# Scores in quarter tiles, a reordered first mixer, 64-column sample products and a third rotation buffer in a two-layer streaming encoder

## The chip, the cores and the metric

The kernel runs on one core of one Trainium2 chip. The core has TensorE (PE; its weight loads are listed as PEld), VectorE (DVE), ScalarE (ACT), GpSimd (POOL) and SyncE (SP). The kernel issues all its DMAs from SP. The metric is device time in microseconds (us) from start to end of one execution; lower is better.

## The reference

One inference step of a two-layer encoder over 1024 prompt frames and 32 sample frames, 1024 features wide. Cut to what matters:

```python
def run_trunk(x, pos, hgrn_state, cache_k, cache_v, ...):
    for layer in range(2):
        h = rms_norm(x, norm_mix_pre[layer])
        if layer == 0:                                   # first mixer
            q, f, i, g = split(h @ w_a_in)               # 4 x 1024 columns
            forget = lb + (1 - lb) * sigmoid(f)
            o, S = hgrn2_scan(silu(q), 1 - forget, i, log(forget), hgrn_state)   # 8 heads
            mix = (rms_norm(o) * silu(g)) @ w_a_out
        else:                                            # second mixer
            k, v = split(rms_norm(x, kv_norm) @ w_kv); k = rope(k, pos)
            q = rope(h @ w_b_q, pos)                     # 16 query heads, 4 key heads
            p = softmax(q @ k / 8 over own and two earlier chunks of 64 keys, with sinks)
            mix = (p @ v) @ w_b_out
        x = x + rms_norm(mix, norm_mix_post[layer])
        a, b = split(rms_norm(x) @ w_ffn_in[layer])      # 2 x 2816
        x = x + rms_norm((silu(a) * b) @ w_ffn_out[layer])
```

A chunk has 64 frames, so a query sees 192 keys: its own chunk and two before it. The outputs are both frame streams, the mixer's states and the newest 128 keys and values.

## The kernel before

**Frames and numbers.** The 1056 frames are three blocks of columns, b = 0, 1, 2, with W = 384, 384 and 288. The last 32 columns of block 2 are the sample. Dense products are made of three: each operand is split into a rounded part and its remainder (`xh`, `xl`, `wh`, `wl`), and xh·wh, xl·wh and xh·wl are summed in PSUM in one accumulation. `wunit` loads 128x1024 weights into `wst` (two buffers), ACT casts them to `wh` (line 102, or 98 with a scale), and DVE subtracts to get `wl` (line 103 or 99).

**Two dense forms.** `mm_fm` (line 141) has weights stationary and W frames moving: 24 matmuls for 128 features. `mm_tm` (line 153) has up to 128 frames stationary and 256 weight columns moving: 24 matmuls. Block 2 calls it for 128, 128 and 32 frames. Products land in the PSUM tag `mm`, which has four slots.

**First mixer.** It starts with `xload(0)`, which casts the first block and sums its squares; `rnorm` (lines 188 and 163 to 171) turns the sums into `rb`, a reciprocal root taken in ten small steps on ACT and DVE; `rcol` (line 201) turns `rb` into columns `rt`. `vproj` and `gproj` make the values and gates with `mm_tm`. For each head, `stage_a` makes F and Q, `stage_b` decays on DVE and POOL, `stage_c` the scores, `states` the states (its transposes `pt`, line 958, need POOL's line 941), `outputs` the outputs. After a block's last gates `oback` transposes all eight heads (`pgt`, line 1026, two PSUM slots); ACT and DVE empty them (lines 1028 and 1029).

**Second mixer.** `rope` makes two products and rotates them on DVE (lines 1129 to 1132) and POOL (1133, 1134) into a tile `ra` with two buffers, which then goes to DRAM as `kd` (keys) or `qd` (queries). `kproj(2)` also writes the two key outputs `out_kp` and `out_ks` from `ra` (lines 1158 and 1159). Attention has 12 units for each block (4 key heads, 3 pieces of 128 frames). A unit is `att_s` (scores, line 1273; row maximum, exponentials), `att_t` (six transposes `ptp`, lines 1333 and 1342) and `att_v` (values, lines 1355 and 1370). A query piece holds two chunks. The keys they share are scored with both chunks as 128 stationary columns, the other 64 keys of each with 64. Between the units stand fillers: late `qproj`s in block 0, `outproj` (output product, norm, next norm) of blocks 0 and 1 in blocks 1 and 2; `postnorm` of block 0 rereads its rows from DRAM (`xo<-xsc`, line 278).

**Order.** The program's text gives priorities; a scheduling layer that weighs costs of its own decides what stands where in each engine's queue, and pools wait for their buffers. An engine works its queue in order.

Of the kernel before, what the change touches and what calls it, by code (L numbers as in the profile page):

```python
# [59 lines left out]
def build(nc, tc, I, O):  # L60
# [82 lines left out]

    def mm_tm(ps, rows, units, xh, xl, t0):
        n = 24
        i = 0
        for u, (wh, wl) in enumerate(units):
            for k in range(4):
# [34 lines left out]

    def rnorm(acc, dst, W, ps=None):
# [5 lines left out]
        rsqrt(dst[:, :W], ps[:, :W], v[:, :W], t[:, :W], ps[:, :W], D,  # L190
              lambda o, x: nc.scalar.activation(o, x, AF.Square),
# [458 lines left out]
    def outproj(b, arr, pre, w2, xold, wnext, spill, ahead=None):  # L650
# [5 lines left out]
        for k in range(KT):  # L656
# [7 lines left out]
            mm_fm(ps, W, units, (k % 2) * 128, lambda q: oh[:, q, :], lambda q: ol[:, q, :])  # L664
# [18 lines left out]
    with tc.tile_pool(name="hp", bufs=1) as hp, \  # L683
# [4 lines left out]
        def xload(b, mid=None):  # L688
# [5 lines left out]
            for k in range(KT):  # L694
# [9 lines left out]
                put_x(b, k, xo[:, :W], xs[b], "mix_pre0")  # L704
                sq_acc(acc, W, xo[:, :W], k == 0)
# [5 lines left out]
            rcol(rb, W, r, hps.tile([128, 512], F32, tag="hs", name="hs", bufs=1) if b == 0 else None)  # L711

        xl0 = xload(0, lambda: first_units.append(wunit(I["wfq"][1])))
# [13 lines left out]
        state = [None] * 8  # L727

        def vproj(p, b, ahead=0):
# [4 lines left out]
            for jl in range(3):  # L734
                rows = min(128, W - jl * 128)
                ps = mmps()
                mm_tm(ps, rows, units, xs[b][0], xs[b][1], jl * 128)
# [7 lines left out]
        v0 = vproj(0, 0, 1)  # L745

        def gproj(p, b):
            units = wpair("wg", p)
            W = BL[b][1]
            for jl in range(3):  # L750
                rows = min(128, W - jl * 128)
                ps = mmps()
                mm_tm(ps, rows, units, xs[b][0], xs[b][1], jl * 128)
# [15 lines left out]
        def stage_a(c, h, b):  # L769
# [16 lines left out]
            if h == b == 0:  # L786
                go(xl0)
                go(v0, 2)
# [251 lines left out]
        for b in range(NB):  # L1040
# [9 lines left out]
            for h in range(8):  # L1050
# [5 lines left out]
                go(ga)  # L1056
                go(gs)
# [9 lines left out]
                if b > 0 and h == 1:  # L1067
                    oback(b - 1)
# [42 lines left out]
    def rope(b, units, res):  # L1111
# [3 lines left out]
        mm_fm(pA, W, units, 0, lambda k: xh[:, k, :], lambda k: xl[:, k, :])  # L1115
        yield
        pB = mmps()
        mm_fm(pB, W, units, 128, lambda k: xh[:, k, :], lambda k: xl[:, k, :])
# [8 lines left out]
        a = rp[0].tile([128, 2, 384], F32, tag="ra", name="ra", bufs=2)  # L1127
# [18 lines left out]
    def kproj(b, units):  # L1146
# [8 lines left out]
        if b < 2:  # L1155
            kload(b)
        else:
            nc.sync.dma_start(O["kp"], a[:, :, 128:256])
            nc.sync.dma_start(O["ks"][:, :, 96:128], a[:, :, 256:288])

    def vproj1(b, units):
# [3 lines left out]
        for jl in range(3):  # L1165
            rows = min(128, W - jl * 128)
            ps = mmps()
            mm_tm(ps, rows, units, xh, xl, jl * 128)
# [16 lines left out]
    def qproj(b, g, units):  # L1185
# [366 lines left out]
```

## Time and profile before

| | us |
|---|---|
| three runs | 2492.41, 2497.97, 2497.51 (median 2497.51) |
| profiled execution | 2499.08 |
| its span, first to last instruction | 2496.6 |
| PE busy in the span | 2426.9 (97%) |
| DVE, ACT, POOL busy | 1695.8 (68%), 1124.0 (45%), 245.5 (10%) |

The profile is of one execution. Its time exceeds its span by 2.5 us, which lie before and after it. A matmul is written with its stationary size (rows*columns) and its moving operand (partitions x columns). Matmuls overlap in the array, so a matmul's duration is not its cost; the distance from one start to the next is. A group's busy time is the time in which at least one of it ran. The granted clock (PEclk) is a share of 2.4 GHz: 0.50 is the lower of the two levels, 1.2 GHz.

### The profile page before, as it was taken

The page shows a single profiled execution, that of the slowest core. Times are in us where ns is not written, and L with a number is a line of the kernel's source. Part 1 is how long each engine was busy: PE and PEld are TensorE (multiplying, and loading weights), DVE is VectorE, ACT ScalarE, POOL GpSimd, SP SyncE. Part 2 cuts the span into 40 slices and gives each one's busy share as a digit, 9 for nine tenths or more (in the row PEclk, how much of TensorE's full clock was granted, in tenths as well). Part 3 has the DMA queues.
Part 4 walks back from the last instruction along what each step waited for, and adds up shares of the span by engine and source line. Part 5 has one row for each costly group of instructions (what it writes and reads, how often), then busy time and mean ns, then how long its engine had stood idle before and what let it go on. Part 6 is the DMA issues. An engine that isn't in the chain of part 4 may idle for free.

```text
span 2496.6 us, 45627 instructions
## 1 busy us (share of the span) xinstructions
PE 2426.9 (97%) x17964; PEld 2361.4 (95%) x17964; DVE 1695.8 (68%) x3733; ACT 1124.0 (45%) x2467; POOL 245.5 (10%) x477
## 2 busy tenths in 40 slices
PE   7999999999999999999999999999999999999997
PEld 7999998998999999999999998887999999999997
DVE  8888779887876666652458846688776666643466
ACT  6555655656543333343235425777433333341333
POOL 3343224231000000000000221000000000000000
PEclk8999999999999999999999999999999999999999
DMA  5332334443522222242346642344422222242455
GB/s 174 94 102 92 119 116 128 125 137 102 169 82 86 78 77 77 77 156 95 129 128 203 194 142 73 103 123 136 135 74 77 77 77 77 75 159 78 153 169 157
DMA packets 125295, 288.93 MB, mean 116 GB/s; under 512 B 13672, under 2 KB 69768, under 8 KB 125080
## 3 DMA queue, kind: packets, MB, share of 16 engines
q1 hardware_dynamic: 125080, 286.03, 36.6%
q8 instruction: 140, 2.29, 0.4%
q14 instruction: 75, 0.61, 0.1%
HBM read 237.05 MB, written 48.07 MB: 114 GB/s over the span
## 4 chain that ended last, share of the span: by engine, by line
PE 74%; DVE 12%; DMA 6%; ACT 5%; issue 2%; POOL 1%; SPq 0%; DVEq 0%; ACTq 0%; POOLq 0%
PE mm L141 25%; PE mm L507 18%; PE mm L416 15%; PE c L416 6%; PE mm L153 5%; DVE wl L103 2%; ACT wh L102 1%; DMA wst<-in_wfo 1%; DVE wl L99 1%; PE sc L1273 1%; DMA wst<-in_wfq 1%; DVE acc L182 1%; PE pav L1355 1%; DMA xl<-g 1%; DMA wst<-in_wk 1%
## 5 line engine op out<-in xcount | busy, mean ns | idle before, releaser
L141 PE MATMUL mm<-xh,wh 128*128 128x384 f32 (+1 forms) x1968 | 630.0, 321 | 12.0 <-ACT xh L220 7.8
L141 PE MATMUL mm<-xh,wl 128*128 128x384 f32 (+1 forms) x1968 | 623.0, 317 | 4.2 <-DVE wl L103 3.3
L141 PE MATMUL mm<-xl,wh 128*128 128x384 f32 (+1 forms) x1968 | 622.7, 317 | 0.5 <-DVE xl L218 0.2
L102 ACT CAST wh<-wst 128x1024 fp32r<-128x1024 f32 (+1 forms) x301 | 314.1, 1046 | 358.9 <-PE mm L507 196.6
L103 DVE TENSOR_TENSOR wl<-wst,wh 128x1024 fp32r<-128x1024 f32 (+1 forms) x301 | 369.2, 1230 | 137.8 <-ACT wh L102 136.4
L141 PEld LDWEIGHTS mm<-xh,wh 128*128 128x128 f32 x1968 | 371.2, 189 | 17.8 <-ACT xh L220 8.0
L141 PEld LDWEIGHTS mm<-xh,wl 128*128 128x128 f32 x1968 | 371.5, 189 | 7.1 <-DVE wl L103 4.7
L141 PEld LDWEIGHTS mm<-xl,wh 128*128 128x128 f32 x1968 | 371.4, 189 | 5.2 <-DVE xl L221 1.5
L507 PE MATMUL mm<-xh,wl 128*128 128x384 f32 (+1 forms) x768 | 246.7, 321 | 2.0 <-DVE wl L103 2.0
L507 PE MATMUL mm<-xh,wh 128*128 128x384 f32 (+1 forms) x768 | 246.6, 321 | 0.0
L507 PE MATMUL mm<-xl,wh 128*128 128x384 f32 (+1 forms) x768 | 246.5, 321 | 0.0
L153 PE MATMUL mm<-wh,xh 128*128 128x256 f32 (+1 forms) x648 | 188.0, 290 | 5.6 <-DVE tmp L1130 4.1
L153 PE MATMUL mm<-wh,xl 128*128 128x256 f32 (+1 forms) x648 | 184.2, 284 | 0.0
L153 PE MATMUL mm<-wl,xh 128*128 128x256 f32 (+1 forms) x648 | 183.8, 284 | 0.0
L400 ACT CAST sh<-sr 128x512 fp32r<-128x512 f32 x144 | 89.5, 622 | 174.9 <-PE mm L416 147.6
L507 PEld LDWEIGHTS mm<-xh,wl 128*128 128x128 f32 x768 | 144.3, 188 | 2.6 <-DVE wl L103 2.5
L507 PEld LDWEIGHTS mm<-xl,wh 128*128 128x128 f32 x768 | 144.1, 188 | 0.0
L507 PEld LDWEIGHTS mm<-xh,wh 128*128 128x128 f32 x768 | 144.1, 188 | 0.0
L153 PEld LDWEIGHTS mm<-wh,xh 128*128 128x128 f32 (+1 forms) x648 | 119.0, 184 | 8.4 <-DVE tmp L1130 4.2
L153 PEld LDWEIGHTS mm<-wh,xl 128*128 128x128 f32 (+1 forms) x648 | 119.1, 184 | 0.8 <-issue 0.2
L153 PEld LDWEIGHTS mm<-wl,xh 128*128 128x128 f32 (+1 forms) x648 | 119.2, 184 | 0.6
L99 DVE SCALAR_TENSOR_TENSOR wl<-wst,pv,wh 128x256 fp32r<-128x256 f32 x160 | 78.7, 528 | 35.2 <-ACT wh L98 34.8
(296 smaller groups left out, 5061.1 us busy)
## 6 DMA issues: line engine op xcount, KB each, us to landing
wst<-in_wfo SPq DMA_DIRECT2D x92, 512.0 KB
wst<-in_wfi SPq DMA_DIRECT2D x88, 512.0 KB
wst<-in_wfq SPq DMA_DIRECT2D x47, 512.0 KB
g<-u SPq DMA_DIRECT2D x72, 192.0 KB
wst<-in_wi SPq DMA_DIRECT2D x24, 512.0 KB
wst<-in_wg SPq DMA_DIRECT2D x24, 512.0 KB
wst<-in_wao SPq DMA_DIRECT2D x24, 512.0 KB
xl<-g SPq DMA_DIRECT2D x32, 384.0 KB
```

What stands on the lines that cost most here:

```text
L99: nc.vector.scalar_tensor_tensor(wl[:, s], st[:, s], pcol(name, k0 + k), wh[:, s].bitcast(F32), mult, sub)
L102: nc.scalar.copy(wh[:, s], st[:, s])
L103: nc.vector.tensor_tensor(wl[:, s], st[:, s], wh[:, s].bitcast(F32), sub)
L141: last_mm[0] = nc.tensor.matmul(ps[:, :W], w, x, start=i == 0, stop=i == n - 1)
L153: last_mm[0] = nc.tensor.matmul(ps[:rows, :256], x, w, start=i == 0, stop=i == n - 1)
L182: nc.vector.tensor_tensor(acc[:, :W], acc[:, :W], q[:, :W], add)
L400: nc.scalar.copy(h, r)
L416: last_mm[0] = nc.tensor.matmul(ps[:, :384], a, c, start=start and k == i == 0, stop=k == 3 and i == 2, skip_group_check=True)
L507: last_mm[0] = nc.tensor.matmul(ps[:, :W], a, c[:, q, :], start=start and q == i == 0, stop=stop and q == f - 1 and i == 2, skip_group_che ...
L1273: nc.tensor.matmul(ps[p0:p0 + m, pr, c0:c0 + w], qts[b, g][rsl, pi, q0:q0 + m], keys[rsl, g, k0:k0 + w], start=True, stop=True, skip_group ...
L1355: nc.tensor.matmul(pav[pr * 64:pr * 64 + 64, pi, :rows], (vc if j == 8 else svs[j])[:, fs], p1[:, pr, pi, :rows], start=True, stop=False, ...
```

## The change

- **Scores in quarters.** Each chunk's 192 keys are scored at once with 64 stationary columns: eight matmuls of 192 columns instead of four of 128 and eight of 64. In `att_v` the full-height products are cut by chunk as well: eight of 64 columns instead of four of 128; the eight of half height stay.
- **Sample as 64 columns.** `pair32` puts xh and xl of the sample side by side (two POOL copies). `mm_tm32` multiplies these 64 stationary columns by wh and by wl: 16 matmuls instead of 24; ACT copies one half out of PSUM and DVE adds the other. It is used in the nine calls of `mm_tm` with 32 rows (four of `vproj`, four of `gproj`, one of `vproj1`).
- **First mixer.** All three value products of the first block stand ahead of `rcol`, not two. The casts of blocks 1 and 2 are issued after the last square of the first `rnorm`. `oback(b - 1)` moves from the end of head 1 to head 2, between that head's F and Q products.
- **Rotation.** `ra` has three buffers in the second part of the rotations, and the key outputs are copied from `kd` in DRAM (`kout`), not from `ra`.
- **Fillers in halves.** `mm_half` issues 12 matmuls, and the generators of fillers stop after each half; a new table spreads 16 halves over 12 units.

```diff
+    def mm_half(ps, W, units, col, ah, al, u):
+        wh, wl = units[u]
+        for k in range(4):
...
+            for i, (w, x) in enumerate(((h, a), (h, b), (l, a))):
+                last_mm[0] = nc.tensor.matmul(ps[:, :W], w, x, start=u == k == i == 0, stop=u == 1 and k == 3 and i == 2)
...
+    def pair32(x, pool):
+        xp2 = pool.tile([128, KT, 64], F32R, name="xlast")
+        for i in range(2):
+            nc.gpsimd.tensor_copy(xp2[:, :, 32 * i:32 * i + 32], x[i][:, :, 256:288])
+        return xp2
+    def mm_tm32(units, xp2):
+        ps = mmps()
+        for kt in range(KT):
+            wh, wl = (w[:, kt % 4 * 256:kt % 4 * 256 + 256] for w in units[kt // 4])
+            for i, w in enumerate((wh, wl)):
+                last_mm[0] = nc.tensor.matmul(ps[:64, :256], xp2[:, kt, :], w, start=kt == i == 0,
+                                              stop=kt == KT - 1 and i == 1)
+        t = tmp()
+        nc.scalar.copy(t[:32, :256], ps[32:64, :256])
+        nc.vector.tensor_tensor(t[:32, :256], t[:32, :256], ps[:32, :256], add)
+        return t
...
-                put_x(b, k, xo[:, :W], xs[b], "mix_pre0")
-                sq_acc(acc, W, xo[:, :W], k == 0)
+                with tc.issue_after(first_chain[0]) if b else nullcontext():
+                    put_x(b, k, xo[:, :W], xs[b], "mix_pre0")
+                    sq_acc(acc, W, xo[:, :W], k == 0)
...
-        v0 = vproj(0, 0, 1)
+        v0 = vproj(0, 0, 2)
...
-                go(v0, 2)
+                go(v0, 3)
...
+                if b > 0 and h == 2:
+                    oback(b - 1)
...
-                if b > 0 and h == 1:
-                    oback(b - 1)
...
-        a = rp[0].tile([128, 2, 384], F32, tag="ra", name="ra", bufs=2)
+        a = rp[0].tile([128, 2, 384], F32, tag="ra", name="ra", bufs=2 if rp[0] is rp1 else 3)
...
-        else:
-            nc.sync.dma_start(O["kp"], a[:, :, 128:256])
-            nc.sync.dma_start(O["ks"][:, :, 96:128], a[:, :, 256:288])
+    def kout():
+        for hf in range(2):
+            for arr, t0, c0, n in (("kp", 0, 128, 128), ("ks", 96, 256, 32)):
+                nc.sync.dma_start(O[arr][:, hf, t0:t0 + n].rearrange("(g r) t -> g r t", g=4),
+                                  kds[2][:, hf, :, c0:c0 + n])
...
+                for p0 in ((0,) if samp else (0, 64)):
...
+                            mm(pr, pi, p0, 64, pi * o2, kb, k0 + p0, 192)
...
+                            for pr in range(2):
+                                pv(pi, pr, cs, svs[j] if ch != pi else vts[j - 1 + ch], al, p1[:, pr, pi, cs],
+                                   ch == 0 or j == pi == 0)
...
+        for f, b, u0 in ((qlate(), 0, 0), (p, 1, 1), (o, 2, 0)):
+            for i in range(16):
+                plan[b][u0 + i * 3 // 4].append((f, 1))
+        plan[1][12].append((p, 2))
```

The order of instructions at three places, before and after:

DVE's queue at the start of the program, from the first step of the first `rnorm` to its last (`rb_236`); `xl_1211` and `xl_3998` are the casts of blocks 1 and 2. Before:

```order
L163 TENSOR_SCALAR rb_236<-nv 128x384
L221 SCALAR_TENSOR_TENSOR xl_3998<-xo,pv,xh_3997 128x288 x2
L221 SCALAR_TENSOR_TENSOR xl_1211<-mixb,pv,xh_1210 128x384
L165 TENSOR_TENSOR tmp<-tmp,nv 128x384
L221 SCALAR_TENSOR_TENSOR xl_1211<-mixb,pv,xh_1210 128x384 x2
L167 TENSOR_TENSOR tmp<-po,tmp 128x384
L221 SCALAR_TENSOR_TENSOR xl_1211<-mixb,pv,xh_1210 128x384
L168 SCALAR_TENSOR_TENSOR rb_236<-tmp,rb_236 128x384
L103 TENSOR_TENSOR wl<-wst,wh 128x1024 x2
L170 SCALAR_TENSOR_TENSOR tmp<-tmp,nv 128x384
L221 SCALAR_TENSOR_TENSOR xl_1211<-mixb,pv,xh_1210 128x384
L171 SCALAR_TENSOR_TENSOR rb_236<-tmp,rb_236 128x384
```

After:

```order
L193 TENSOR_SCALAR rb_236<-nv 128x384
L195 TENSOR_TENSOR tmp<-tmp,nv 128x384
L197 TENSOR_TENSOR tmp<-po,tmp 128x384
L198 SCALAR_TENSOR_TENSOR rb_236<-tmp,rb_236 128x384
L103 TENSOR_TENSOR wl<-wst,wh 128x1024
L200 SCALAR_TENSOR_TENSOR tmp<-tmp,nv 128x384
L255 SCALAR_TENSOR_TENSOR xl_1211<-mixb,pv,xh_1210 128x384
L201 SCALAR_TENSOR_TENSOR rb_236<-tmp,rb_236 128x384
```

Seven casts of later blocks stood within the chain; one does now. Two weight subtractions stood ahead of line 170; one does now.

PE's queue at one attention unit of block 0: a filler's matmul, the scores (`sc`), the transposes (`ptp`), the next filler matmul. Before:

```order
L141 MATMUL mm<-xh_15969,wh 128x384
L1273 MATMUL sc<-kb,qt 128x128 x4
L1273 MATMUL sc<-kb,qt 64x64 x8
L1333 MATMUL ptp<-ident,P 128x128 x4
L1342 MATMUL ptp<-ident,P 128x128 x2
L141 MATMUL mm<-xl_15970,wh 128x384
```

After:

```order
L152 MATMUL mm<-xh_16425,wl 128x288
L1333 MATMUL sc<-kb,qt 64x192 x8
L1387 MATMUL ptp<-ident,P 128x128 x4
L1396 MATMUL ptp<-ident,P 128x128 x2
L152 MATMUL mm<-xh_16425,wh 128x288
```

Two shapes of scores became one (the size printed is that of the output).

SP's queue where `kproj(2)` ends: `ra_17028` (after: `ra_16991`) holds its rotated keys, `in_wq` are weights of later queries, `qd2_0` the next rotation's result. Before:

```order
L1193 DMA qd1_0_16945<-ra_16936 4x32x384 x2
L91 DMA wst_17230<-in_wq 128x1024
L1154 DMA kd2_17037<-ra_17028 4x32x288 x2
L1158 DMA out_kp<-ra_17028 256x1x128
L1159 DMA out_ks<-ra_17028 256x1x32
L91 DMA wst_17242<-in_wq 128x1024
L91 DMA wst_17442<-in_wq 128x1024
```

After:

```order
L1254 DMA qd1_0_16908<-ra_16899 4x32x384 x2
L91 DMA wst_17189<-in_wq 128x1024
L1209 DMA kd2_17000<-ra_16991 4x32x288 x2
L91 DMA wst_17201<-in_wq 128x1024
L1216 DMA out_kp<-kd2_17000 128x1x128
L1254 DMA qd2_0_17062<-ra_17053 4x32x288 x2
L91 DMA wst_17401<-in_wq 128x1024
L1238 DMA out_vp<-vt_17148 128x256
L91 DMA wst_17413<-in_wq 128x1024
L1240 DMA out_vs<-vt_17174 32x256
L1216 DMA out_ks<-kd2_17000 128x1x32
```

The key outputs now read `kd2_17000`, so SP waits for the landing of `kd2` ahead of the first of them; one weight load moved ahead of it, and `qd2_0` and the later weight loads stand behind it.

## Rows read from the trace of the kernel before

**Rows 1.** Windows: us; busy of PE, PEld, DVE, ACT, POOL; clock, DMA share, GB/s

```profile
62.00:620.00 558.00, 546.60 (x4981) 527.71 (x4977) 461.82 (x1426) 326.35 (x854) 183.44 (x392) 1.00 0.37 113
...
1440.00:1502.00 62.00, 57.29 (x373) 56.81 (x372) 27.07 (x60) 14.11 (x34) 11.03 (x12) 0.97 0.48 142
1502.00:1735.00 233.00, 222.77 (x2502) 188.14 (x2502) 174.48 (x496) 169.86 (x557) 10.98 (x10) 0.99 0.34 101
```

**Rows 2.** Waits of PE by releaser: us in all, times, longest us

```profile
PE mm L188 <- DVE acc L182: 7.8, 4, 3.7
PE pgt L1026 <- DVE xl L1029: 4.6, 2, 3.0
PE hs L201 <- DVE rb L171: 4.2, 1, 4.2
PE mm L153 <- DVE tmp L1130: 4.1, 1, 4.1
...
PE pt L958 <- POOL K L941: 2.8, 1, 2.8
```

**Rows 3.** Windows just behind four of PE's waits, columns as in rows 1

```profile
28.20:34.60 6.40, 5.64 (x27) 5.55 (x28) 4.61 (x11) 4.53 (x7) 1.57 (x3) 0.50 0.26 86
52.60:58.50 5.90, 5.90 (x20) 5.90 (x21) 4.59 (x18) 2.73 (x7) 1.10 (x4) 0.50 0.00 0
...
1454.40:1458.00 3.60, 2.94 (x14) 2.94 (x15) 2.70 (x8) 1.71 (x4) 0.00 (x0) 0.53 0.65 210
1710.40:1714.00 3.60, 3.58 (x23) 2.63 (x23) 2.05 (x8) 2.11 (x10) 0.00 (x0) 0.53 0.54 184
```

**Rows 4.** Timeline of PE, a sample product: start, duration (us), operation

```profile
492.46 0.27 PE L153 MATMUL mm<-wl,xh 128*128 128x256 f32 x1
492.57 0.28 PE L153 MATMUL mm<-wh,xh 128*32 128x256 f32 x1
...
495.31 0.30 PE L141 MATMUL mm<-xh,wh 128*128 128x288 f32 x1
```

**Rows 5.** Timeline of PE, the scores of one unit

```profile
1510.37 1.11 PE L1273 MATMUL sc<-kb,qt 64*128 64x128 f32 x24
1511.40 0.44 PE L141 MATMUL mm<-xh,wl 128*128 128x384 f32 x1
1511.68 0.34 PE L141 MATMUL mm<-xh,wh 128*128 128x384 f32 x1
```

**Rows 6.** Timeline of PE, the values of one unit

```profile
1594.64 0.66 PE L1355 MATMUL pav<-p,sv 128*64 128x128 f32 x8
1595.23 0.27 PE L1370 MATMUL pav<-p,vt 64*64 64x64 f32 x1
...
1595.33 0.22 PE L1370 MATMUL pav<-p,vt 64*64 64x64 f32 x1
...
1595.45 0.22 PE L1370 MATMUL pav<-p,sv 64*64 64x64 f32 x1
```

**Rows 7.** Timeline of PE, two groups of a decay product

```profile
44.28 0.72 PE L927 MATMUL psB<-ZZ,K 128*64 128x96 f32 x12
44.83 0.51 PE L930 MATMUL psB<-Q,K 128*64 128x64 f32 x6
```

**Rows 8.** Timeline of DVE and of SP's queue at the key rotation

```profile
1454.18 0.46 DVE L1129 TENSOR_TENSOR ra<-mm,cosr 128x288 f32<-128x288 f32 x1 [7.30 <-DMA qd<-ra]
...
1450.69 2.35 SPq L1159 DMA_DIRECT2D out_ks<-ra  x1
1453.14 4.81 SPq L91 DMA_DIRECT2D wst<-in_wq  x2
```

**Rows 9.** Timeline of DVE, first and last step of the first root

```profile
18.70 0.36 DVE L163 TENSOR_SCALAR rb<-nv 128x384 int32<-128x384 int32 x1
...
27.32 0.56 DVE L171 SCALAR_TENSOR_TENSOR rb<-tmp,rb 128x384 f32<-128x384 f32 x1
```

**Rows 10.** Chain of work through PE's wait at 1706.7: start, us, what

```profile
1704.91 3.67 DMA xo<-xsc
```

More of the change, by code (lines that the diff above doesn't have):

```diff
@@ L648, in build, with outproj @@
     nx = [None] * NB
-    def outproj(b, arr, pre, w2, xold, wnext, spill, ahead=None):
+    def outproj(b, arr, pre, w2, xold, wnext, spill, ahead=None, halves=False):
         W = BL[b][1]
@@ L663, in outproj @@
             ps = mmps()
-            mm_fm(ps, W, units, (k % 2) * 128, lambda q: oh[:, q, :], lambda q: ol[:, q, :])
+            for u in range(2):
+                mm_half(ps, W, units, (k % 2) * 128, lambda q: oh[:, q, :], lambda q: ol[:, q, :], u)
+                if halves and u == 0:
+                    yield
             nc.scalar.copy(mix[:, k, :W], ps[:, :W])
@@ L735, in vproj @@
                 rows = min(128, W - jl * 128)
-                ps = mmps()
-                mm_tm(ps, rows, units, xs[b][0], xs[b][1], jl * 128)
+                if rows == 32:
+                    ps = mm_tm32(units, xlast[0])
+                else:
+                    ps = hps.tile([128, 512], F32, tag="hsc", name="pv", bufs=2) if ahead == jl == 2 else mmps()
+                    mm_tm(ps, rows, units, xs[b][0], xs[b][1], jl * 128)
                 pss.append((jl, rows, ps))
@@ L1109, in take, with rope @@
         xs[b], rts[b], rbs[b] = res[b]
-    def rope(b, units, res):
+    def rope(b, units, res, halves=False):
         W = BL[b][1]
@@ L1114, in rope @@
         pA = mmps()
-        mm_fm(pA, W, units, 0, lambda k: xh[:, k, :], lambda k: xl[:, k, :])
-        yield
+        for u in range(2):
+            mm_half(pA, W, units, 0, lambda k: xh[:, k, :], lambda k: xl[:, k, :], u)
+            if halves or u:
+                yield
         pB = mmps()
-        mm_fm(pB, W, units, 128, lambda k: xh[:, k, :], lambda k: xl[:, k, :])
+        for u in range(2):
+            mm_half(pB, W, units, 128, lambda k: xh[:, k, :], lambda k: xl[:, k, :], u)
+            if halves and u == 0:
+                yield
         if cosin[b] is None:
@@ L1166, in vproj1 @@
             rows = min(128, W - jl * 128)
-            ps = mmps()
-            mm_tm(ps, rows, units, xh, xl, jl * 128)
+            if rows == 32:
+                ps = mm_tm32(units, pair32(xs[b], rp[0]))
+            else:
+                ps = mmps()
+                mm_tm(ps, rows, units, xh, xl, jl * 128)
             if jl == 0:
@@ L1183, in build, with qproj @@
     qds = {}
-    def qproj(b, g, units):
+    def qproj(b, g, units, halves=False):
         W = BL[b][1]
         r = []
-        yield from rope(b, units, r)
+        yield from rope(b, units, r, halves)
         a = r[0]
@@ L1352, in att_v, with pv @@
             pav = aps.tile([128, 2, 512], F32, tag="pt", name="pav", bufs=1)
-            for pi in range(2):
-                for pr in range(2):
-                    nc.tensor.matmul(pav[pr * 64:pr * 64 + 64, pi, :rows], (vc if j == 8 else svs[j])[:, fs],
-                                     p1[:, pr, pi, :rows], start=True, stop=False, skip_group_check=True)
+            def pv(pi, pr, cs, vt, rsl, m, first):
+                nc.tensor.matmul(pav[pr * 64:pr * 64 + 64, pi, cs], vt[rsl, fs], m, start=first, stop=True,
+                                 skip_group_check=True)
+            al = slice(0, 128)
             if j == 8:
@@ L1425, in build @@
                 kload(2)
+                kout()
                 close(rpc)
```

98 lines of the change are left out of this document (55 added, 43 removed).

## The prediction, made before the changed kernel ran

> **What bounds the kernel now.** I read the table of busy times first: TensorE works 2426.9 of 2496.6 us, VectorE 1695.8. So the time is TensorE's work plus some 70 us of its idle time, and a gain must be either work that TensorE loses or a wait of TensorE that goes. The windows by stage show where the two lie [rows 1]: in the first mixer TensorE is busy 546.6 of 558 us (and DVE 461.8 of them, 83%), around the rotations 57.3 of 62, in attention 222.8 of 233. Then I read TensorE's waits by releaser. Five kinds touch the change [rows 2]: a norm's sum (line 188, 3.7 at the longest), `oback`'s transposes (1026), the first `rcol` (201), a product behind the rotation (153) and the first `pt` (958). Last I read what follows a wait. In four stretches that begin right behind one of these waits, the granted clock is 0.50 to 0.53, the 1.2 GHz level, where the stages have 0.97 to 1.00 [rows 3]. So a wait costs more than its length.
>
> I estimate that surcharge from the same windows. At 2.4 GHz a 128x256 product starts every 0.12 us (492.46, 492.57) [rows 4]; in the window at 28.2 TensorE was busy 5.64 us at half clock. Work that the columns limit would have taken half of it; from this I count 2 to 3 us for each of the two long windows at the start, and 1.7 for each of the two windows of 3.6 us. Whether a removed wait also returns its surcharge depends on whether some smaller wait stays there.
>
> **The change part by part**, against this execution's own 2499.1 us. It lies 1.6 above the median of the runs, so I take about 1 off at the end.
>
> *Sample as 64 columns.* From the first 128x32 matmul at 492.57 to the next product at 495.31 are 2.74 us for 24 matmuls, 0.114 each, and the product of 128 stationary columns ahead of it has 0.12 or less [rows 4]. So the number of stationary columns hardly sets the distance; the 256 moving ones do. Sixteen matmuls at 0.114 to 0.12 are 1.82 to 1.92, a gain of 0.82 to 0.92, nine times: 7.4 to 8.2. The new copy on ACT and sum on DVE lie behind the next product's matmuls, except once: the last block's last gate product has `oback` behind it, where the chain grows by about 1 us if nothing covers it. The copies of `pair32` are on POOL, early and far ahead of their first use. I take -7.5.
>
> *Scores.* A unit's scores occupy TensorE from 1510.37 to 1511.40, 1.03 us [rows 5]. (Each float matmul is two rows here: 24 rows for 12 matmuls.) The new form is 16 rows, four sets of four 64x64 tiles. Sets of 64 columns run side by side and start every 0.06 us (1595.33 to 1595.45, two sets) [rows 6]; 192 columns are three times as many, about 0.174 a set, 0.70 in all. A change of tile shape costs about 0.1: the filler at 1511.40 is followed by the next after 0.28 instead of 0.17 [rows 5]. With 0.16 for the changes I get 0.86, a gain of 0.17 in each of 28 units of full pieces: -4.8.
>
> *Values.* The four full-height matmuls, eight rows of 128 columns, take 0.59, until 1595.23 [rows 6]; less 0.15 for the change of shape that is 0.11 for two rows side by side. Twelve rows with 96 columns last 0.72 from first start to last end; without one row's own 0.22 [rows 6] that is 0.045 a step, 0.09 for two [rows 7]. By the same step of 0.02 two rows of 64 columns take 0.07. The lower bound is one such row alone: six last 0.51 [rows 7], 0.058 a step. Eight pairs are then 0.46 to 0.56, with 0.15 for the change 0.61 to 0.71: 0.02 to 0.12 more than now, 0.6 to 3.4 in 28 units. I take +1.5; that they go in pairs I take from the old ones, which do in the same two halves of the array. Scores and values together: -3.3, with ends -1.4 and -4.2.
>
> The Trainium skill, in "TensorEngine Tiling (Array Packing)", section "Instruction Overhead", puts about 60 cycles on each matmul. By an estimate from that page the eight further rows of values cost 8 x 25 ns = 0.2 us a unit, 5.6 in all, and the two edits together would be about +0.8; no row here shows such an addition where tiles run side by side, and the sum goes by the rows.
>
> *Rotation.* DVE stood 7.30 us before line 1129 at 1454.18, until the DMA out of `ra` had read it [rows 8], and TensorE 4.1 behind it [rows 2]. With a third buffer that wait goes. But SP's queue is the second limit: in it the two writes of key outputs and the weight loads stand one behind another (1450.69 for 2.35 us, 1453.14 for 4.81) [rows 8]. Now the key outputs read what `kd` wrote, so SP waits for `kd` to land, and `qd2_0` and the later weights stand behind it; one weight load went ahead, which speaks for the change. Those weights feed the casts of the next queries; if they come late, TensorE waits for them. The wait (4.1) and the half-clock window at 1454.4 (1.7) make -5.8; I leave 0.8 for late weights: -5, with ends -3 and -6.5.
>
> *Start.* The root's chain on DVE runs from 18.70 to 27.88 (27.32 + 0.56) [rows 9], and TensorE waits 4.2 us for it at `rcol` [rows 2]. Six of the seven foreign casts and one of two subtractions leave it, so that I expect its end at 25 to 25.7; and the third value product, 24 x 0.12 = 2.9 us, moves into the gap. Together these close it. What is late next: the casts of later blocks come after the chain, when DVE and POOL make the first decays; `psA`, `psB` and the `pt` whose wait on POOL is 2.8 us at 52.5 [rows 2] are wanted some 4 us earlier by TensorE, and are only partly earlier themselves. I take -4, with ends -2 and -8 (the latter if the windows at 28.2 and 52.6 [rows 3] return to full clock).
>
> *`oback` moved.* `pgt` wait 4.6 us for DVE's line 1029 in two cases [rows 2], since they stand right behind the last gate product and two PSUM slots must be emptied. Behind head 2's F they have at least 51 matmuls, over 6 us at 0.12 [rows 4], between that product and themselves. I take all of it, -4.6; the other end is 0 (the emptying waits equally there, because DVE is 83% busy).
>
> *Fillers in halves.* TensorE's longest wait in attention is 3.7 us at line 188 [rows 2]: a norm's sum stands in DVE's queue behind line 278, which waits for rows being reread from DRAM, 3.67 us on the chain [rows 10]. Halves spread the filler, so the reread can be issued earlier relative to its use, and more filler stands beside each softmax; but DVE's order still holds the sum behind those rows. I take -2.5, ends 0 and -5.4 (3.7 and the 1.7 behind it [rows 3]).
>
> The sum: -7.5 - 3.3 - 5 - 4 - 4.6 - 2.5 = -26.9, so 2472.2 by this execution, and near **2471** as a median.
>
> **The rivals.**
>
> *Waits move, not vanish.* DVE is busy 83% of the first mixer and 75% of attention (174.5 of 233) [rows 1]. If what waited for DVE is only asked for earlier, start, `oback` and fillers return little; left are 7.5 + 3.3 and about half of the rotation, 2.5, or -13.3: 2486. For it speaks that each of the five waits but one is for DVE; against it that two of them have a foreign queue entry or a missing buffer as cause, which the change takes away.
>
> *The clock comes back too.* If no wait stays at these places, the four windows [rows 3] run at 2.4 GHz, and the upper ends hold: start -8, `oback` -4.6, fillers -5.4, rotation -6.5, with 10.8 for the rest: -35.3, 2464; with the other three waits of line 188, 4.1 together [rows 2], which lie on like paths, 2460. The rows show the lower level only behind waits of 2.8 us and more. "TensorE: Matmul & The Clock Gate" of the Trainium skill, section "HAM Oscillation", has it likewise that an idle stretch brings the gate back; the trace agrees with its four windows at 0.50 to 0.53. Against it: line 188's and 958's waits have causes that stay.
>
> *The sample's columns save nothing.* Sixteen matmuls with 64 stationary columns at 0.171 would take 2.74 again: -19.4, 2479. Only rows of 32 and 128 stationary columns exist, and both speak against it.
>
> *Quarter tiles do not run side by side (other side).* All rows of four tiles at once [rows 6] have 64 columns. If with 192 columns each of the 16 rows of scores waits for the one before, a unit has 16 x 0.174 = 2.8 instead of 1.03, +1.8 in 28 units: +50 against -4.8 assumed, and the time is 2472 + 55, about 2525. It decides, and the kernel is slower, from a loss of about 1 us a unit, which is a pairing of tiles instead of a fourfold one (8 x 0.174 + 0.16 = 1.55, +0.5 a unit, would still leave about 2490).
>
> **How the numbers follow.** About 0.3%, 7.5 us, is what a measurement of this kernel tells from no change: faster is below 2490, slower above 2505. Chances: my sum with its waits partly gone, 2463 to 2479: 0.55; moved waits, 2480 to 2488: 0.20; the clock too, 2455 to 2463: 0.15; the sample without gain: 0.04; lost overlap: 0.03; gains eaten by new waits in SP's queue or at the start so that nothing is left, 2490 to 2500: 0.03. The time is that of the likeliest, 2471. A range from 2455 to 2488 holds the first three cases and the fourth, up to a part of the tails of each: the low end is the sum of the best ends (-8.2, -4.2, -6.5, -8, -4.6, -5.4 and the 4.1 of line 188: 2458) less the run's offset and a little, the high end the moved waits with the rotation at nothing. Faster 0.91, the same 0.06 (the last case, half of lost pairing and the tail of the moved waits), slower 0.03.
>
> **What the changed profile would show.** Sample: the stretch of 128x256 products with 64 stationary columns 1.8 to 1.9 us long, at line 153's successor. Scores: 0.8 to 0.9 us a unit, values 1.0 to 1.15. Rotation: no wait of DVE for a DMA out of `ra`, and SP waiting for `kd` ahead of the first key output; wrong, if ACT's casts of the next query weights wait over 3 us more than now. Start: no wait at `rcol`, the root done by 25.7; wrong, if `psA`, `psB` or `pt` wait together over 4 us before 60. `oback`: no `pgt` in TensorE's waits above 0.5 us. Fillers: the wait at line 188 under 2 us; wrong if it stays at 3.7. The prediction as a whole fails if scores take over 1.5 us a unit, or if TensorE's busy time falls by less than 8 us.

## The result and the profile after

The changed kernel takes 2482.4 us (median of 4 runs, 2480.28 to 2483.85) against 2497.74 before (4 runs): ratio 0.994, 95% interval 0.9927 to 0.9952. It is faster by 15.3 us, 0.6%. The time lies in the range, but 11 us above the 2471 forecast, outside the likeliest case (2463 to 2479) and within that of moved waits (2480 to 2488), which had a chance of 0.20. The profiled execution took 2480.28 us with a span of 2478.5, 18.1 shorter than the span of before.

The windows by stage (length; busy time of PE, PEld, DVE, ACT, POOL; clock; DMA share; GB/s), answering to [rows 1]:

```profile
0.00:62.00 62.00, 51.67 (x429) 49.58 (x430) 53.61 (x130) 40.93 (x86) 26.87 (x54) 0.97 0.52 167
62.00:620.00 558.00, 544.26 (x4933) 526.02 (x4932) 472.38 (x1441) 337.25 (x877) 176.00 (x385) 1.00 0.37 117
...
1440.00:1502.00 62.00, 56.54 (x382) 54.48 (x383) 28.76 (x73) 18.32 (x52) 11.85 (x13) 0.97 0.36 113
```

The stages have moved against each other, so these shares only say where TensorE still idles: in the rotations it is busy 56.5 of 62 us, no more than before. The waits of PE by releaser, answering to [rows 2], say on what:

```profile
...
PE mm L179 <- DVE ra L1187: 5.3, 1, 5.3
...
PE mm L220 <- DVE acc L212: 4.4, 4, 1.6
PE pgt L1076 <- DVE xl L1079: 3.2, 2, 1.9
PE pu L1016 <- ACT kT L1010: 3.2, 2, 2.0
PE ptp L1387 <- DVE P L1370: 2.7, 7, 0.5
PE ptp L1387 <- DVE xl L1438: 2.7, 6, 0.6
PE psB L977 <- ACT K L882: 2.6, 1, 2.6
```

The first `rcol` and `pt` are gone from the list. The norm's sum (now line 220) fell from 7.8 to 4.4. `pgt` fell only from 4.6 to 3.2, the wait behind the rotation grew from 4.1 to 5.3. `psB` is new, and two kinds grew: `pu` from 1.1 to 4.3 and the transposes `ptp` from 2.2 to 5.4, each added up over its releasers.

Where the time went along the program is read from starts of the same work in both timelines. `psA` of head 1 began at 60.57 before and now at 52.45, 8.1 earlier; `psA` of head 4 at 124.47 and now

```profile
119.37 0.62 PE L963 MATMUL psA<-XX,K 128*32 128x80 f32 x24
```

so only 5.1 earlier. The list by stages, worked out from such pairs: start 8.1 earlier, 3.3 of it lost by head 7 of block 0; 0.6 won at the first `oback`; 6.4 between head 7 of block 1 and the first norm of the feed-forward stage, while eight sample products there save 7.0; 0.4 lost at the rotation; 2.3 won in attention; the rest, some 4 us, lies mostly in the two feed-forward stages, which no edit touches and which differ by up to 3 us between the profiles of these kernels.

### The profile page after: what moved, and what is told of

Read it like the earlier page. It is cut to its first block, busy times and chain, and to the rows that moved or that the text cites. A ratio compares the mean times of both kernels' runs of the same rounds, so it can differ in the third digit from the quotient of the medians.

```text
span 2478.5 us, 45524 instructions
## 1 busy us (share of the span) xinstructions
PE 2411.6 (97%) x17908; PEld 2343.8 (95%) x17908; DVE 1696.1 (68%) x3742; ACT 1125.4 (45%) x2476; POOL 245.2 (10%) x481
## 4 chain that ended last, share of the span: by engine, by line
PE 71%; DVE 14%; DMA 5%; ACT 5%; issue 2%; POOL 1%; SPq 0%; ACTq 0%; DVEq 0%; POOLq 0%
PE mm L541 18%; PE mm L141 18%; PE mm L450 15%; PE c L450 6%; PE mm L152 6%; PE mm L163 4%; DVE wl L103 2%; ACT wh L102 1%; ACT P L1362 1%; DVE wl L99 1%; PE pav L1408 1%; DVE acc L212 1%; DVE at L944 1%; DMA wst<-in_wao 1%; DMA wst<-in_wfo 1%
## 5 line engine op out<-in xcount | busy, mean ns | idle before, releaser
L141 PE MATMUL mm<-xh,wh 128*128 128x288 f32 (+1 forms) x1344 | 422.5, 315 | 9.3 <-ACT xh L254 7.4
L141 PE MATMUL mm<-xh,wl 128*128 128x288 f32 (+1 forms) x1344 | 418.4, 312 | 5.0 <-DVE wl L103 4.9
L141 PE MATMUL mm<-xl,wh 128*128 128x288 f32 (+1 forms) x1344 | 417.8, 311 | 0.7 <-DVE xl L255 0.3
L141 PEld LDWEIGHTS mm<-xl,wh 128*128 128x128 f32 x1344 | 253.1, 188 | 3.1 <-DVE xl L255 1.3
L541 PE MATMUL mm<-xh,wl 128*128 128x384 f32 (+1 forms) x768 | 246.6, 321 | 1.9 <-DVE wl L103 1.8
L541 PE MATMUL mm<-xh,wh 128*128 128x384 f32 (+1 forms) x768 | 246.6, 321 | 0.0
L541 PE MATMUL mm<-xl,wh 128*128 128x384 f32 (+1 forms) x768 | 246.5, 321 | 0.0
L152 PE MATMUL mm<-xh,wh 128*128 128x384 f32 (+1 forms) x624 | 207.0, 332 | 0.9 <-DVE tmp L1185 0.5
L152 PE MATMUL mm<-xh,wl 128*128 128x384 f32 (+1 forms) x624 | 202.8, 325 | 2.1 <-DVE wl L99 1.1
L152 PE MATMUL mm<-xl,wh 128*128 128x384 f32 (+1 forms) x624 | 203.8, 327 | 0.0
L163 PE MATMUL mm<-wh,xh 128*128 128x256 f32 x568 | 165.0, 291 | 0.7 <-DVE rt L237 0.7
L163 PE MATMUL mm<-wh,xl 128*128 128x256 f32 x568 | 161.2, 284 | 0.0
L163 PE MATMUL mm<-wl,xh 128*128 128x256 f32 x568 | 161.0, 284 | 0.0
L541 PEld LDWEIGHTS mm<-xl,wh 128*128 128x128 f32 x768 | 144.1, 188 | 0.0
```

The costliest lines, as they stand in the source:

```text
L141: last_mm[0] = nc.tensor.matmul(ps[:, :W], w, x, start=i == 0, stop=i == n - 1)
L152: last_mm[0] = nc.tensor.matmul(ps[:, :W], w, x, start=u == k == i == 0, stop=u == 1 and k == 3 and i == 2)
L541: last_mm[0] = nc.tensor.matmul(ps[:, :W], a, c[:, q, :], start=start and q == i == 0, stop=stop and q == f - 1 and i == 2, skip_group_che ...
```

## The experiments

All are variants of the changed kernel and were timed beside the kernel before on one chip each (its medians there: 2499.6 to 2501.3).

**The changed kernel once more.**

> The changed kernel once more, unaltered, beside the other three: its ratio to the kernel before should lie between 0.992 and 0.995, and its trace should show which of the differences between single profiles (up to 2 us in stretches that no edit touches) are chance.

Measured: 2483.15 us, ratio 0.9936 (0.9922 to 0.995). Its profile differs from the first by up to 1.7 us on the way (head 1 begins at 54.18) and by 0.3 at the end. This is the size of chance in a single profile. One profile below (the casts) even has 2.5 us more in an attention that its edit does not touch, 250.0 us; in the nine other profiles with this attention, the first one included, the stretch lasts 247.0 to 247.9.

**Rotation undone.**

```diff
-        a = ... tag="ra", name="ra", bufs=2 if rp[0] is rp1 else 3)
+        a = ... tag="ra", name="ra", bufs=2)
...
+        else:
+            nc.sync.dma_start(O["kp"], a[:, :, 128:256])
+            nc.sync.dma_start(O["ks"][:, :, 96:128], a[:, :, 256:288])
...
-                kout()
```

> The changed kernel with the rotation undone: two ra buffers, key outputs written from ra, as before. My theory now: TensorE's wait behind the rotation (5.3 us in the changed kernel, 4.1 before) is not set by ra but by DVE's queue, where the subtractions (line 99) of query weights that have not landed stand ahead of the second half of the rotation, so this run should give the changed kernel's time within 2 us (2480 to 2485), with a wait of 4 to 5.5 us in the same place. The prediction's theory, that the third buffer removes a wait of 4 to 6 us: then this run is 4 to 6 us slower, 2486 to 2489.

Measured: 2483.64, ratio 0.9927 (0.9912 to 0.9942): the edit is worth nothing. The wait stands there with either number of buffers; only the releaser's name differs. PE in this run:

```profile
1444.32 0.58 PE L163 MATMUL mm<-wh,xh 128*128 128x256 f32 x1 [5.13 <-DVE tmp L1185]
```

and ACT, in the changed kernel, waits for weights, with DVE's subtractions behind it:

```profile
1441.93 1.70 ACT L98 ACTIVATE wh<-wst,pv 128x256 fp32r<-128x256 f32 x4 [13.39 <-DMA wst<-in_wq]
```

```profile
1430.67 0.44 DVE L1184 TENSOR_TENSOR ra<-mm,cosr 128x288 f32<-128x288 f32 x1
...
1442.47 1.68 DVE L99 SCALAR_TENSOR_TENSOR wl<-wst,pv,wh 128x256 fp32r<-128x256 f32 x4 [11.01 <-ACT wh L98]
1444.07 0.45 DVE L1186 TENSOR_TENSOR tmp<-mm,sinr 128x288 f32<-128x288 f32 x1
1444.44 0.45 DVE L1187 TENSOR_TENSOR ra<-mm,cosr 128x288 f32<-128x288 f32 x1
```

DVE's wait for `ra` ahead of the first half (line 1184) is gone, as predicted. DVE could have done the second half (lines 1186 and 1187) long before too; it stands behind the subtraction of weights that have not landed. Two causes remain: DVE's order, or the weights. The next three runs separate them.

**DVE's order alone.**

```diff
+                with tc.issue_after(hold[0]) if hold[0] else nullcontext():
+                    nc.vector.scalar_tensor_tensor(wl[:, s], ...)
...
+        rot20 = rot_end[0]
...
+        hold[0] = rot20
         uq = wq(1)
+        hold[0] = None
```

> The changed kernel with one change in DVE's queue: the first subtractions of the second query group's weights are put behind the last step of the rotation of block 2's first queries. Theory (DVE's queue order): the wait of 5.3 us ahead of the sample's value product goes, and the product starts right behind the one before. What is late next are the weights themselves (their halves ready at about 1444.2 and 1448.5), so that only 2 to 3.5 us of the time are won: 2479 to 2481. Rival (the rotation waits for something else, ra or a PSUM slot): no change within 1 us. Rival 2 (the weights' landing alone decides when the next query product can start): the wait moves to that product and nothing is won.

Measured: 2483.3, ratio 0.9932 (0.9917 to 0.9948). My theory fell and the second rival has it: the sample's product follows without a wait, and TensorE then waits for the weights themselves, a little longer:

```profile
1452.46 0.66 PE L155 MATMUL mm<-xh,wh 128*128 128x384 f32 x1 [6.43 <-ACT wh L100]
```

**The layout alone.** Rotated keys and queries lie in DRAM as 128 rows for each half instead of 4 groups of 32; the reads are split.

```diff
-        kd = kds[b] = tc.dram_tile([4, 2, 32, W], F32, name=f"kd{b}")
+        kd = kds[b] = tc.dram_tile([2, 128, W], F32, name=f"kd{b}")
...
-            nc.sync.dma_start(kd[:, hf], a[:, hf, :W])
+            nc.sync.dma_start(kd[hf], a[:, hf, :W])
...
-        qd = qds[b, g] = tc.dram_tile([2, 2, 2, 32, W], F32, ...)
+        qd = qds[b, g] = tc.dram_tile([2, 128, W], F32, ...)
...
-            nc.sync.dma_start(qd[:, :, hf].rearrange(...), a[:, hf, :W])
+            nc.sync.dma_start(qd[hf], a[:, hf, :W])
```

> The changed kernel with another DRAM layout of rotated keys and queries: each write covers 128 consecutive rows instead of 4 groups of 32, and the reads are split in two or four. In the changed kernel the packets of these writes flow at a quarter of the DMA share (0.25 to 0.27 from 1440 to 1444), and the weights issued at 1433.3 and 1435.8 land 8.6 and 10.4 us later. Theory: these writes occupy few of the 16 DMA engines, and the weights' last packets queue behind them; spread out, the weights land 3 to 5 us earlier and the time falls by 3 to 5 us: 2477 to 2480. Rival (the late issue on SP or the bandwidth sets the landing): landing earlier by less than 1 us and the time within 1 us of the changed kernel; with the added reads on SP it could be 1 to 2 us slower.

Measured: 2473.53, ratio 0.9891 (0.9875 to 0.9908): some 10 us less than the changed kernel, twice what I expected, and the fastest version here. In the changed kernel the chain of waits runs over the weights' transfer,

```profile
1435.83 10.42 DMA wst<-in_wq
```

and while TensorE stands idle the DMA engines are busy a quarter of the time (windows, columns as above):

```profile
1440.00:1444.00 4.00, 0.00 (x0) 0.00 (x0) 1.52 (x4) 1.70 (x4) 0.00 (x0) 1.00 0.27 99
```

With whole rows ACT casts the same weights nearly 7 us earlier. SP's queue, changed kernel and this run, shows when the first of them was issued:

```profile
1433.29 0.44 SPq L91 DMA_DIRECT2D wst<-in_wq  x1
```

```profile
1430.85 0.52 SPq L91 DMA_DIRECT2D wst<-in_wq  x1
```

```profile
1435.12 1.71 ACT L98 ACTIVATE wh<-wst,pv 128x256 fp32r<-128x256 f32 x4 [5.56 <-DMA wst<-in_wq]
```

So of the 6.8 us, 2.4 are an earlier issue, and the rest is a faster landing: ACT begins 4.3 us after the issue instead of 8.6. The earlier issue has two causes in SP's queue. In the changed kernel's chain SP waits 4.55 us for a write of `qd` from 1422.21 before it reads that back, and two reads of `xo` and two more writes of `qd` stand ahead of the weights (1430.34 to 1433.19); in this run they stand elsewhere. So the edit also reordered SP's queue, and no run separates that from the layout.

The list of DMA issues gives 3.7 us in the median from issue to landing for all eight loads of these weights (last column), and the window over the rotations has TensorE almost without a gap:

```profile
wst<-in_wq SPq DMA_DIRECT2D x8, 512.0 KB, 3.7
```

```profile
1440.00:1502.00 62.00, 61.12 (x462) 58.32 (x461) 30.20 (x79) 19.03 (x58) 11.67 (x12) 1.00 0.38 122
```

TensorE is busy 61.1 of 62 us there instead of 56.5, at full clock. From the last norm before to attention's first scores the program is 8.2 us shorter than in the changed kernel: the wait of 5.3, the lower clock behind it (0.58 from 1445.0 to 1448.5, where the sample's sixteen matmuls started over 3.09 us instead of 1.75), and smaller waits for weights after it. A rule of the Trainium skill, on its page "DMA: Bandwidth & Descriptors", section "Rules for kernel authors", names what the share shows: a transfer is spread over as many of the 16 DMA engines as its slowest dimension allows, so an outermost dimension of 4 confines it to 4. The share of 0.27 agrees. The DMA packets kept in the trace agree too. From 1440.5 to 1443.5 of the changed kernel 4.3 packets are in flight at a time in the mean, most of them of 1152 bytes, which is one row of 288 floats; with whole rows packets of this size fly up to 18 at a time. The weights' packets, of 4096 bytes, stop at 1441.4 and come again at 1443.1, a few at a time until 1445.6, so the last ones do come behind the narrow writes. The trace does not name the engine of a packet.

The layout was run only on top of the third buffer; what the third buffer is worth when the weights are in time was not tried.

**Both.**

> The two edits together: DVE's rotation ahead of the late subtractions, and the writes of rotated keys and queries over all rows. If both theories hold, the wait behind the rotation is under 0.5 us and the next query product waits for weights under 1 us, 5 to 7 us less than the changed kernel: 2475 to 2477. If the weights' landing alone decides, this run equals the one with the layout alone; if the order alone decides, it equals the one with the order alone.

Measured: 2474.69, ratio 0.9893 (0.9876 to 0.9909), the same as with the layout alone. So the weights decide: the order of DVE's queue won nothing with late weights and wins nothing with early ones.

**Sample undone:** three calls of `mm_tm32` replaced by `mm_tm` for 32 rows.

> The changed kernel with the sample's products as 24 matmuls of 32 stationary columns again. If TensorE sets the pace there, each of the eight products of the first mixer takes 2.74 instead of 1.87 us and the time rises by 7.0 us (0.28%), 2488 to 2491; the ninth, behind the rotation, adds nothing, because the weights that come next are late anyway. Rival (DVE sets the pace of the first mixer, 83% busy): the waits shrink as the products grow and only 2 to 4 us are lost.

Measured: 2491.68, ratio 0.9964 (0.9951 to 0.9977). That is 8.5 us above the changed kernel's 2483.15 of another series, or 7.0 by the two ratios: the first theory. In the changed kernel's timeline of PE the product runs from its first to the next product's first matmul in 1.87 us, 0.117 each:

```profile
485.58 0.28 PE L179 MATMUL mm<-wh,xlast 128*64 128x256 f32 x1
...
487.45 0.30 PE L141 MATMUL mm<-xh,wh 128*128 128x288 f32 x1
```

**Scores and values undone** (`att_s` and `att_v` of before), and **fillers undone** (whole products and the table of before).

> The changed kernel with scores and values of before. In the changed kernel a unit's scores hold TensorE 0.81 instead of 1.04 us and its values 1.01 instead of 0.98, about 5.7 us less in all units, but the stretch from the first scores to the norm behind attention became only 2.3 us shorter, and the steps into the transposes (from scores or fillers) hold 9 us more. Theory (softmax on DVE and ACT sets the pace, so that what TensorE saves in scores it waits for at the transposes): this run is 0 to 2 us slower than the changed kernel, and its waits at the transposes are 4 to 6 us shorter. Rival (the waits come from the fillers in halves): the stretch gets 5 to 6 us longer.

> The changed kernel with whole filler products and their table of before, the quarter scores kept. Theory (softmax sets the pace): the time stays within 2 us of the changed kernel; the wait of 3.7 us at line 188 of before comes back, and about as much goes at the transposes. Rival (the halves cause the new waits at the transposes, 9 us, and take 2.9 from the norm's sum): 5 to 7 us faster, 2476. Third possibility (the halves hid work): 3 to 5 us slower.

Measured: scores undone 2484.05, ratio 0.9933 (0.9919 to 0.9946); fillers undone 2486.62, ratio 0.995 (0.9937 to 0.9963). The stretch from the first scores to the norm behind attention, as one window of each kernel: before, then the changed kernel, scores undone, fillers undone:

```profile
1502.61:1752.51 249.90, 239.67 (x2624) 205.28 (x2624) 189.09 (x522) 182.10 (x580) 10.98 (x10) 0.99 0.37 112
```

```profile
1488.67:1736.24 247.57, 235.61 (x2639) 197.47 (x2639) 187.99 (x521) 180.15 (x580) 10.10 (x10) 1.00 0.37 113
```

```profile
1490.65:1741.81 251.16, 242.13 (x2623) 205.18 (x2623) 187.97 (x521) 180.41 (x579) 10.15 (x10) 0.99 0.37 111
```

```profile
1490.03:1740.57 250.54, 237.66 (x2640) 200.76 (x2640) 189.42 (x521) 181.56 (x580) 10.99 (x10) 0.99 0.37 112
```

From before to after TensorE's busy time falls by 4.1 us, its idle time rises from 10.2 to 12.0. Each half undone gives back all of the 2.3 won, and a little more; so neither half alone shortened this stretch. But by chance alone the same attention gave 250.0 in one profile, and the timed runs don't tell scores undone from the changed kernel at all; fillers undone is 3.5 us slower, with intervals that still touch. So the theory that softmax sets the pace is not shown by these two; what is shown is that attention gave at most some 3 us, with either part of it unresolved.

One expectation for the fillers missed outright. With whole fillers and the old table the wait of 3.7 us for the norm's sum does not come back: at 1693.91 that product starts without a wait, and so it does with the scores undone (1703.54). Instead the values just ahead wait for DVE, 1.9 and 2.9 us. So it is not shown that the halves removed the sum's wait; it may only have moved.

**The post-norm's addition on POOL,** together with the layout.

```diff
-            nc.vector.tensor_tensor(m, m, xos[k][:, :W], add)
+            (nc.gpsimd if wnext == "ffn_pre1" else nc.vector).tensor_tensor(m, m, xos[k][:, :W], add)
```

> The changed kernel with the layout of rotated keys and queries in whole rows (1% under the kernel before in an earlier run) and, in the second mixer's post-norms, the addition of the old stream (line 286) on POOL instead of DVE, some 9 us of DVE's work in blocks 1 and 2 of attention. If DVE's load sets the pace of attention, the waits at the transposes and values fall and the stretch from the first scores to the norm behind attention gets 2 to 4 us shorter than with the layout alone: ratio 0.987 to 0.988. Rival (the softmax's own chain, or ACT, sets it): no change of that stretch, ratio 0.989; if POOL's slower additions delay the next norm, 1 to 2 us longer.

Measured: 2482.97, ratio 0.9936 (0.9923 to 0.9948), 9 us worse than the layout alone. Attention's stretch is 257.4 us, 9.5 more than with the layout alone; PE waits 6.8 for `p` (line 1402) instead of 2.0. So this did not try a lighter DVE: with 8.4 us of additions taken from it, it was busier in the stretch (190.2 against 187.9 us); the last section shows why. How much of the 9.5 us comes from that, and whether DVE's load sets attention's pace, stays open.

**`oback` in two groups of four heads,** the first where it stood before the change.

```diff
                 if b > 0 and h == 2:
-                    oback(b - 1)
+                    oback(b - 1, range(4, 8))
...
+                if b > 0 and h == 1:
+                    oback(b - 1, range(4))
```

> The changed kernel with oback in two parts: the first four heads at the end of head 1, as before the change, the other four between head 2's F and Q. Theory: the transposes wait because their two PSUM slots are emptied by DVE in a queue that is over 80% busy, eight in a row, not because of the last gate product; two groups of four need only two emptied slots each, so that the waits (3.2 us in all) fall to about 1 and the time by 1 to 2.5 us: 2480 to 2481. Rival (what is waited for is the last gate product's way through DVE, as the prediction had it): the first group waits as before the change, 1.5 to 3 us more than now.

Measured: 2484.0, ratio 0.9933 (0.992 to 0.9945), no change; my theory of too few slots fell. The third head's transposes wait in the changed kernel, and with the split first group the longer:

```profile
437.95 0.90 PE L1076 MATMUL pgt<-ident,oraw 128*128 128x128 f32 x3 [1.89 <-DVE xl L1079]
```

```profile
433.18 0.55 PE L1078 MATMUL pgt<-ident,oraw 128*128 128x128 f32 x3 [3.41 <-DVE xl L1081]
```

In the split run DVE works without a gap from before 428 to 432.57, on decays, weights and the gates' roots, before it comes to the two emptied slots. In the changed kernel ACT, too, comes to them only at 436.32, 2.2 us after the transposes. The wait is for the backlog of the two engines that empty the slots, and some of it stays wherever the transposes stand. The rival's sign did come: the first groups wait 1.58 and 3.41 us, as before the change (1.58 and 3.04), and all `pgt` 5.6 instead of 3.2. So the new place does shorten the wait, but 2.4 us more of it did not show in the time.

**The start: the casts put back** (no `issue_after`), and **the third value product put back** (`vproj(0, 0, 1)`, `go(v0, 2)`).

> The changed kernel with the casts of blocks 1 and 2 issued where they were before, within the first root's chain; the third value product stays ahead. Theory (the start is won by the shorter chain and by the product in the gap about equally, and some 3 of its 8 us are given back by block 0's later waits in any case): the first decay product of head 1 begins 1 to 3 us later than in the changed kernel, and at head 8 only 0 to 2 us of that are left; the time within 2 us of the changed kernel. Rival (the casts were the whole cause): 4 to 5 us slower.

> The changed kernel with two value products ahead of the first rcol, as before; the casts stay behind the chain. The chain ends at 26.0 in the changed kernel, and the second product at about 23.5, so that TensorE waits some 2 to 2.5 us at rcol, and the third product comes after it: 3 us later at head 1 if nothing else waits there. If block 0 gives back what TensorE wins at its start (the changed kernel's lead falls from 8.1 at head 1 to 4.8 at head 7), then less than 1.5 us are left at head 8 and in the time; rival: all 3 us stay.

Measured: 2482.68, ratio 0.9936 (0.9922 to 0.995), and 2483.7, ratio 0.9935 (0.9921 to 0.9949): both equal to the changed kernel. In the third's run TensorE waits again at `rcol` and begins head 1 3.6 us later than in the changed kernel, but head 4 only 0.6:

```profile
27.16 0.83 PE L235 MATMUL hs<-ident,rb 128*128 128x1 f32 x6 [2.45 <-DVE rb L201]
...
119.99 0.62 PE L963 MATMUL psA<-XX,K 128*32 128x80 f32 x24
```

With the casts put back head 4 begins at 119.19. With either half left out, head 4 begins as with both: in eleven profiles with the whole edit at the start it begins between 118.3 and 121.2, before the change at 124.47. These eleven fall into two groups. Eight begin head 1 at 52.2 to 53.5 and then wait 1.7 to 2.3 us at `pu`; three begin it at 54.2 to 54.4 and wait 0.4 us there or less. A start that is won by more than some 6 us is given back at `pu`. The kernel with both halves left out was not run.

## Why the prediction was right and where not

**Sample, right.** Predicted 1.82 to 1.92 us for each product and 7.5 in all; measured 1.87, and 7.0 to 8.5 by undoing it. With 256 moving columns the distance of matmuls is 0.114 to 0.12 us at 32, 64 and 128 stationary ones.

**Scores and values, right in the units, wrong in the time.** Scores take 0.82 (predicted 0.86), values 1.01 (from 1599.83 to 1600.84), 0.03 more than before (predicted 0.02 to 0.12):

```profile
1636.26 0.88 PE L1333 MATMUL sc<-kb,qt 64*64 64x192 f32 x16
1637.08 0.44 PE L152 MATMUL mm<-xh,wh 128*128 128x384 f32 x1
```

If all units are like these, that is 28 x 0.21 - 28 x 0.03 = 5.0 us, more than the 3.3 taken. Lost overlap of quarter tiles did not come. By the prediction's estimate from the Trainium skill ("TensorEngine Tiling (Array Packing)", section "Instruction Overhead") the eight further rows would have cost 0.2 us a unit; the rows show 0.03. By the same estimate the scores, with eight rows fewer, would have gained as much, so the +0.8 given there for both edits does not follow from it.

**Fillers, partly.** The sum's wait did fall, to 0.74 (1696.16), from 3.7 [rows 2], but that the halves did it is not shown: with the fillers undone the sum does not wait either. And the two terms for attention, 5.8 together, gave 2.3. The step that failed is that TensorE's saved time is time saved: the transposes now wait where TensorE came later before (5.4 us at `ptp` against 2.2). This is the rival "waits move", with the open point named above of what they wait for in the end.

**Rotation, wrong.** The step "with a third buffer that wait goes" failed. DVE's wait for the DMA out of `ra` did go, but TensorE's did not: 5.3 us after, 4.1 before, and the stretch from the last norm to attention lost 0.4 instead of winning 5. Before, two waits ended close together. DVE's for `ra` ended at 1454.18 [rows 8], and I priced it as the whole. The other was ACT's, for the weights, in the same microseconds:

```profile
1455.36 1.71 ACT L98 ACTIVATE wh<-wst,pv 128x256 fp32r<-128x256 f32 x4 [12.59 <-DMA wst<-in_wq]
```

I left 0.8 us for late weights; the price was the whole 5. The sign that I set for them could not show it: the casts wait 13.39 us after, only 0.8 more, because they were late already. What makes them late, writes of 4 groups of rows, stands in both kernels, and the case that SP's queue eats the gain had a chance of 0.03 for the whole kernel.

**Start, right in size, for another reason.** Predicted 4; 8.1 won at head 1, with the windows at 28.2 and 52.6 at full clock (1.00 and 1.00 instead of 0.50 [rows 3]), as in the rival of the clock (a shorter stretch at 0.69 came in from 40.2 to 44.0, behind the wait at `psB`); then 3.3 lost by head 7; in the second profile 6.4 and 0.8. The root ended at 26.1, not by 25.7. A wait of 2.65 at `psB` for ACT's `K` comes ahead of head 1. The largest wait behind it is `pu`:

```profile
118.50 0.71 PE L1016 MATMUL pu<-vt,kT 128*128 128x128 f32 x4 [1.97 <-ACT kT L1010]
```

On ACT `kT` stands there behind a step of block 1's root that waits for DVE. That head 4 begins at nearly the same time in all these profiles fits a limit that ACT and DVE set in block 0, so that either half of the edit did nearly as well as both.

**`oback`, wrong.** Predicted 4.6, won some 0.4 over two blocks (0.6 at the first, -0.2 at the second). The failed step is that distance from the last gate product takes all of the wait: it fell only from 4.6 to 3.2. The other end of the bounds, emptying that "waits equally there, because DVE is 83% busy", was nearer.

**The sum.** Against this span: sample 7.0, attention 2.3, rotation -0.4, start 4.8, `oback` 0.4, together 14.1 of 26.9 predicted; the remaining 4 of the 18.1 lie mostly in stages without an edit, and repeated timing gives 15 to 16 in all. That the time is within the range owes much to the range's width of 33 us. Its nearness to 2486 is partly luck: the case of moved waits counted half of the rotation, which gave nothing, and little of the start, which gave 4.8.

## What to carry to other kernels

A wait that the profile gives to one releaser may hide a second that ends a microsecond later (here 1454.18 and 1455.36): before pricing a removed wait, read what every other engine waits for in the same microseconds, and its DMAs. TensorE's lead is worth only what the engines behind it can follow; a lead of 8 us shrank to 5 within four heads. And the DRAM layout of a write can decide when loads beside it land: with 4 groups of 32 rows the weights came 8.6 us after their issue, with 128 rows 4.3.

## What the runs showed of the hardware that was not expected

Additions on POOL slowed DVE. By groups of lines from 1640 to 1735, the layout alone first, then with the additions on POOL:

```profile
L212 DVE TENSOR_TENSOR acc<-acc,tmp 128x384 f32<-128x384 f32 x18 | 9.8, 546 | 0.1
L285 DVE SCALAR_TENSOR_TENSOR mixb<-mixb,pv,rb 128x384 f32<-128x384 f32 x12 | 7.1, 606 | 0.0
L1356 DVE TENSOR_REDUCE rm<-sc 128x2 f32<-128x384 f32 x12 | 6.1, 545 | 0.7 <-PE sc L1337 0.7
```

```profile
L212 DVE TENSOR_TENSOR acc<-acc,tmp 128x384 f32<-128x384 f32 x20 | 12.8, 640 | 2.1 <-ACT tmp L211 2.1
L285 DVE SCALAR_TENSOR_TENSOR mixb<-mixb,pv,rb 128x384 f32<-128x384 f32 x10 | 7.9, 838 | 0.0
L1356 DVE TENSOR_REDUCE rm<-sc 128x2 f32<-128x384 f32 x12 | 6.2, 549 | 2.0 <-PE sc L1337 2.0
```

DVE's operations with two SBUF inputs grow from 546 to 640 ns and from 606 to 838 in the mean, while the maximum that reads PSUM stays at 545 to 549. One operation shows it alone: `rs` (line 1369, 128x4, both inputs in SBUF) takes 0.16 us in the median, and 0.97 at 1638.29 in the second run, where two additions of POOL last from 1635.43 to 1639.24.

The Trainium skill has this on the page "SBUF — State Buffer", section "SBUF: two separate sides": POOL and such DVE operations share a port pair that one of them holds at a time. The rows agree. So here POOL was no free help to a busy DVE on SBUF data.
